# Attention in a two-layer backbone: sink as a PSUM column, two query blocks in one value product

## The chip, the core and the metric

One core of a Trainium2 chip runs the whole program in one launch. The metric is device time in microseconds, the median of several runs. The profile shows one execution.

## The reference, cut to what matters

```python
def _sink_softmax(scores, sink):
    snk = sink[:, :, None]
    m = snk
    for s in scores:
        m = jnp.maximum(m, jnp.max(s, axis=-1))
    ex = [jnp.exp(s - m[..., None]) for s in scores]
    denom = jnp.exp(snk - m)
    for e in ex:
        denom = denom + jnp.sum(e, axis=-1)
    return [e / denom[..., None] for e in ex]

def _window_attn_mixer(h, hc, rope, w_in, w_out, q_norm_w, k_norm_w, sink, need_ctx_out):
    ...
    s_win = jnp.einsum('bnqhgd,bnkhd->bnhgqk', qb, kw).astype(f32) * scale
    s_win = jnp.where(valid[None, :, None, None], s_win, -jnp.inf)
    s_ctx = jnp.einsum('bnqhgd,bkhd->bnhgqk', qb, kc).astype(f32) * scale
    p_win, p_ctx = _sink_softmax([s_win, s_ctx], snk)
    o = (jnp.einsum('bnhgqk,bnkhd->bnqhgd', p_win.astype(v.dtype), vw)
         + jnp.einsum('bnhgqk,bkhd->bnqhgd', p_ctx.astype(vc.dtype), vc))
    y = o.reshape(B, L, D_MODEL) @ w_out
```

512 latent tokens in 4 blocks of 128 attend to the 256 context tokens and, in a window of 128 to either side, to their own and the neighbouring blocks. 16 query heads of 64 share 4 key-value heads. Each head has one sink logit, which enters the softmax's maximum and its denominator and has no value. Everything is float32.

## The kernel before

The program runs layer 0 (retention and mLSTM), its FFN, then layer 1: the attention this text is about, its output projection (`op_out`) and a last FFN. All work is written as generators; `Flow` books each instruction with a price by engine and shape (`Engine`, lines 97 to 133) and lets the generator go on that is due first, and the framework's scheduler sets the final order of each engine's queue when the program is built. So a price in `Engine` moves instructions wherever a shape of that kind occurs: for float32 products other than transposes this is line 115. The products of the adaLN modulation (`ada_round`, tile `ada`, weights of 32 columns, fed by the weight tiles `aw`) are float32 too; those outside the start have 256 columns of data.

The attention runs while the main generator still projects queries (`pt`), norms and rotates them (`norm_rope`, transposes `ntr`, results `qst`); keys are `khh` and `kll` (a high and a low part), values `vt`. The loop `its` has 32 items n: 4 key-value groups g, 2 pairs of heads hp, 4 query blocks j. An item has two heads q.

`attention_p` (lines 1952 to 1983) makes one head's probabilities. A two-bank PSUM tile `sc` (two exist, tag `s2`) takes the scores: columns 256 to 511 the context, from 512 on the two or three key blocks of the window, with two products that add the masks. DVE reduces the negated scores to their minimum with the negated sink, ACT takes the exponential with that as bias and sums it, takes the exponential of the sink logit, DVE adds the two sums and inverts, POOL multiplies the tile `aE` (7 exist) by the inverse.

`attention_o` (lines 1985 to 2033) has the rest. PE transposes the probabilities of both heads, 128 columns at a time, into a bank `atr`; ACT or DVE copies two key blocks of it to a tile `pth`, of which there are 5. An item takes 2 or 3 of them (context blocks, then the window's), so that a pair of query blocks needs all 5. After every second item the value product `ao` runs for the pair (lines 2019 to 2025). Its weights are a key block of `vt`, 64 columns, and its data 256 columns: both heads of one query block. Query block j-1 writes the first 64 partitions of the bank and block j the others, each with as many products as it has key blocks (4 and 5, or 5 and 4):

```python
        for i in range(5):
            for s, prs in enumerate(two):
                if i < len(prs):
                    pe.matmul(po[64 * s:64 * s + 64, 0:256], prs[i][0], prs[i][1], start=(i == 0),
                              stop=(i == len(prs) - 1), tile_position=(0, 64 * s))
```

Four copies of 64x128 on ACT (`oh`, the high part) and four subtractions on DVE (`ol`, the low part) then put it into place for the output projection.

Of the kernel before, what the change touches and what calls it, by code (L numbers as in the profile page):

```python
# [96 lines left out]
class Engine:  # L97
# [5 lines left out]
    def __getattr__(self, op):  # L103
        fn = getattr(self._e, op)

        def call(*a, **k):
            r = fn(*a, **k)  # L107
            n = math.prod(a[0].shape[1:])
            if self._n == "pe":
                if op == "transpose":  # L110
                    cost = 0.11
                else:
                    dt, m = a[1].dtype, math.prod(a[1].shape[1:])
                    if dt == F32:
                        cost = max(0.22, 0.01 + n / 600)
                    elif dt == F32R:
                        cost = max(0.106 if m > 64 else 0.054, n / 2400 + 0.003)
                    else:
                        cost = max(0.04, n / 2400 + 0.003)
            elif self._n == "act":  # L120
                cost = 0.095 + n / 1200
            elif self._n == "dve":
                cost = 0.13 + n / 960
            elif ALU.pow in a:
                cost = 0.3 + n / 6
            else:
                cost = 0.3 + n / 600
            if self._n == "pe" and self._f.cur.name == "main":
                self._f.main = r
            self._f.charge(self._n, cost)  # L130
            return r

        return call
# [10 lines left out]
def kernel(ctx, tc, x, c, cx, c_ctx, ada_w, ada_b, norm_w, ffn_w_in, ffn_w_out, ab_w_in,  # L144
# [48 lines left out]
    def f(ap):  # L193
        return ap.bitcast(F32)
# [1625 lines left out]
    n_aE, n_pt = Count(7), Count(5)  # L1820
# [4 lines left out]
    def start1():  # L1825
# [7 lines left out]
        A["sink8"] = sink8 = mt1("sink8", [P, 16], 1)  # L1833
        nc.scalar.dma_start(sink8, sink[0].partition_broadcast(P))
        A["nsink"] = nsink = mt1("nsink", [P, 16], 1)
        dve.tensor_scalar(nsink, sink8, -1.0, None, ALU.mult)
# [110 lines left out]
    E, halfway = {}, {}  # L1947
# [4 lines left out]
    def attention_p(n, g, hp, j, q):  # L1952
# [9 lines left out]
        ps = psum2("sc")  # L1962
# [8 lines left out]
        st = mt1("ast", [P, 5], 7)  # L1971
        e_ = mt1("aE", [P, 640], 7)
        sc = ps[:, NCX:NCX + nk]

        dve.tensor_scalar(e_[:, 0:nk], sc, -1.0, A["nsink"][:, h:h + 1], ALU.mult, ALU.min, accum_out=st[:, 0:1])
        n_sc[0] += 1
        act.activation(e_[:, 0:nk], sc, AF.Exp, bias=st[:, 0:1], accum_out=st[:, 1:2])
        act.activation(st[:, 2:3], A["sink8"][:, h:h + 1], AF.Exp, bias=st[:, 0:1])
        yield
        dve.tensor_tensor(st[:, 3:4], st[:, 1:2], st[:, 2:3], ALU.add)  # L1980
        dve.reciprocal(st[:, 4:5], st[:, 3:4])
        pool.tensor_tensor(e_[:, 0:nk], e_[:, 0:nk], st[:, 4:5].to_broadcast([P, nk]), ALU.mult)
        E[n, q] = e_

    def attention_o(n, g, hp, j):

        kt = 2 * g + hp
        j0, j1 = window(j)
        nb = 2 + j1 - j0
# [6 lines left out]
        yield spend((n_pt, -(-nb // 2)))  # L1996
        pts = []
        for i0 in range(0, nb, 2):
            m = min(2, nb - i0)
            pst = psum("atr", "pj")  # L2000
            for i in range(m):
                for q in range(2):
                    pe.transpose(pst[:, 256 * i + P * q:256 * i + P * q + P],
                                 E[n, q][:, P * (i0 + i):P * (i0 + i) + P], ident)
            pv = pst[:, 0:256 * m].rearrange("p (i n) -> p i n", i=m)
            th = mt1("pth", [P, 2, 256], 5)
            (act.copy if i0 != 2 else dve.tensor_copy)(th[:, 0:m, :], pv)
            pts += [th[:, i, :] for i in range(m)]
            if i0 + 2 < nb:
                flow.cur.t = 0.0  # L2010
                yield
        n_tr[0] += 1
        n_aE.n += 2
        chs = [0, 1] + [2 + jj for jj in range(j0, j1)]
        halfway[n] = [(A["vt"][:, ch, 64 * g:64 * g + 64], pts[i]) for i, ch in enumerate(chs)]
        if j % 2 == 0:
            return
        yield lambda: n_av[0] == n - 1
        po = psum("ao", "mx")
        two = halfway[n - 1], halfway[n]  # L2020
        for i in range(5):
            for s, prs in enumerate(two):
                if i < len(prs):
                    pe.matmul(po[64 * s:64 * s + 64, 0:256], prs[i][0], prs[i][1], start=(i == 0),
                              stop=(i == len(prs) - 1), tile_position=(0, 64 * s))
        n_pt.n += sum(-(-len(prs) // 2) for prs in two)
        n_av[0] += 2
        quads = [(slice(64 * q, 64 * q + 64), slice(P * (j - 1 + s), P * (j + s)),
                  po[64 * s:64 * s + 64, P * q:P * q + P]) for s in range(2) for q in range(2)]
        for r, od, p_ in quads:  # L2030
            act.copy(oh_[kt // 3][r, kt % 3, od], p_)
        for r, od, p_ in quads:
            dve.tensor_tensor(ol_[kt // 3][r, kt % 3, od], p_, f(oh_[kt // 3][r, kt % 3, od]), ALU.subtract)

    def start_attention():
        for n, it in enumerate(its):
            for q in range(2):
                flow.add(attention_p(n, *it, q), 10, f"attention p {n} {q}")
            flow.add(attention_o(n, *it), 10, f"attention o {n}")
# [364 lines left out]
```

## Time and profile before

| | us |
|---|---|
| median of 3 runs (1773.08 to 1778.31) | 1775.1 |
| the profiled execution | 1772.4 |
| its span | 1770.6 |
| PE busy | 1704.5 |
| DVE busy | 1248.5 |
| ACT busy | 774.0 |
| POOL busy | 302.7 |

The span runs from the first to the last instruction of the profiled execution. PE is the engine of the matrix products and transposes; a float32 product shows as two rows there. A busy share is a mean over stages with different limits, so the share of one stage is taken from its own stretch. Starts of neighbouring rows say more of PE than the length of one row, as products are pipelined. In the groups, "idle before" is the time for which the engine stood still ahead of such an instruction, with what ended most of it.

### The profile page before, as it was taken

To read this page: it belongs to the slowest core of one execution; us is meant where nothing else is said; L and a number is where in the kernel's file an instruction comes from. 1 tells how busy PE (TensorE), PEld (TensorE's weight loads), DVE (VectorE), ACT (ScalarE), POOL (GpSimd) and SP (SyncE) were. 2 spreads that over 40 slices of the span, in tenths; PEclk is the share of its full clock that TensorE was granted. 3 is DMA by queue.
4 is the path that set the end of the run, shared out by engine and by line. 5 is a ranking of instruction groups with operands and counts; after the bars stand their busy time and mean duration, and the time that the engine had idled before them with its cause. 6 is when DMAs were issued, how large, how long until landed. Compare 5 with 4: busy or idle time off the path is not lost.

```text
span 1770.6 us, 31626 instructions
## 1 busy us (share of the span) xinstructions
PE 1704.5 (96%) x12738; PEld 1553.7 (88%) x12738; DVE 1248.5 (71%) x2224; ACT 774.0 (44%) x1502; POOL 302.7 (17%) x307
## 2 busy tenths in 40 slices
PE   7899999999998999999999999998999999999998
PEld 5799899999878998989999997897667999999998
DVE  5845365756598886867567566878886687778775
ACT  4532344433324533433334334545675553434343
POOL 4212120201123001010000103435553300000000
PEclk8999999999999999999999999999999999999999
DMA  9511111011476248484656755221002523323335
GB/s 345 197 52 48 37 37 48 25 39 52 161 237 204 83 144 177 126 187 141 166 134 175 167 176 151 84 73 49 1 1 80 171 72 97 119 83 108 108 89 150
DMA packets 230326, 203.36 MB, mean 115 GB/s; under 512 B 8172, under 2 KB 207268, under 8 KB 230180
## 3 DMA queue, kind: packets, MB, share of 16 engines
q1 hardware_dynamic: 222468, 178.20, 33.0%
q0 software_dynamic: 5760, 18.88, 5.5%
q10 hardware_dynamic: 1952, 4.27, 0.7%
q8 instruction: 100, 1.64, 0.4%
q14 instruction: 46, 0.38, 0.1%
HBM read 178.25 MB, written 23.07 MB: 114 GB/s over the span
## 4 chain that ended last, share of the span: by engine, by line
PE 64%; issue 13%; DVE 11%; DMA 6%; ACT 3%; POOL 1%; SPq 0%; POOLq 0%; ACTq 0%; DVEq 0%
PE pf L107 21%; PE pu L107 11%; PE pt L107 10%; PE pg L107 4%; DMA wr<-in_ffn_w_in_dram 3%; PE sc L107 3%; PE pc L107 3%; PE ao L107 2%; DVE wl L107 2%; PE mo L107 2%; PE atr L107 2%; DMA xs<-stage 1%; DVE acc L107 1%; PE ro L107 1%; DMA aw<-in_ada_w_dram 1%
## 5 line engine op out<-in xcount | busy, mean ns | idle before, releaser
L107 PE MATMUL pf<-fu,wh 128*128 128x512 f32 (+1 forms) x1152 | 290.6, 343 | 8.3 <-DVE xt L107 3.8
L107 PEld LDWEIGHTS pf<-fu,wh 128*128 128x128 f32 x1152 | 196.6, 188 | 37.8 <-issue 4.4
L107 ACT CAST wh<-wr 128x1024 fp32r<-128x1024 f32 (+1 forms) x144 | 143.6, 1001 | 179.4 <-PE pf L107 77.7
L107 DVE TENSOR_TENSOR wl<-wr,wh 128x1024 fp32r<-128x1024 f32 (+1 forms) x144 | 174.3, 1212 | 64.6 <-ACT wh L107 62.9
L107 PE MATMUL pf<-fu,wl 128*128 128x512 f32 (+1 forms) x576 | 195.3, 341 | 0.4 <-DVE wl L107 0.4
L107 DVE TENSOR_TENSOR wl<-ws,wh 128x1024 fp32r<-128x1024 f32 x80 | 97.4, 1221 | 57.4 <-ACT wh L107 49.6
L107 PE MATMUL pu<-g,wh 128*128 128x256 f32 x704 | 130.4, 283 | 0.0
L107 ACT CAST xh<-wr 128x1024 fp32r<-128x1024 f32 x84 | 78.4, 946 | 114.3 <-DMA wr<-in_ffn_w_in_dram 61.3
L107 PE MATMUL pc<-g,xh 128*128 128x256 f32 x672 | 122.4, 282 | 1.2 <-ACT stage L107 0.8
L107 ACT CAST wh<-ws 128x1024 fp32r<-128x1024 f32 x80 | 83.3, 1049 | 88.2 <-PE pu L107 45.9
L107 PEld LDWEIGHTS pf<-fu,wl 128*128 128x128 f32 x576 | 108.2, 188 | 14.1 <-DVE wl L107 0.6
L107 DVE SCALAR_TENSOR_TENSOR acc<-aw,cmod,acc 128x1024 f32<-128x1024 f32 x90 | 118.0, 1336 | 0.3
L107 PE MATMUL pu<-hT,wh 128*128 128x256 f32 x640 | 115.4, 281 | 0.0
L107 PEld LDWEIGHTS pu<-g,wh 128*128 128x128 f32 x704 | 108.9, 190 | 1.2 <-issue 1.2
L107 PEld LDWEIGHTS pc<-g,xh 128*128 128x128 f32 x672 | 103.4, 189 | 2.1 <-ACT stage L107 1.2
L107 DVE TENSOR_TENSOR xl<-wr,xh 128x1024 fp32r<-128x1024 f32 x84 | 91.6, 1095 | 18.8 <-ACT xh L107 18.8
L107 PE MATMUL pu<-g,wl 128*128 128x256 f32 x352 | 99.4, 284 | 0.8 <-DVE wl L107 0.8
L107 PEld LDWEIGHTS pu<-hT,wh 128*128 128x128 f32 x640 | 97.6, 188 | 0.6 <-ACT hT L107 0.2
L1774 POOL DMA_DIRECT2D xs<-stage x32 | 27.9, 871 | 393.9 <-ACT stage L107 375.1
L107 PE MATMUL pc<-g,xl 128*128 128x256 f32 x336 | 94.3, 281 | 0.0
L107 PE MATMUL pu<-hT,wl 128*128 128x256 f32 x320 | 88.0, 281 | 0.9 <-DVE wl L107 0.9
L107 PE MATMUL pt<-wh,hh 128*128 128x256 f32 x288 | 83.5, 291 | 3.6 <-ACT hh L107 2.2
(383 smaller groups left out, 4914.7 us busy)
## 6 DMA issues: line engine op xcount, KB each, us to landing
wr<-in_ffn_w_in_dram SPq DMA_DIRECT2D x88, 512.0 KB, 3.9
aw<-in_ada_w_dram SPq DMA_DIRECT2D x84, 512.0 KB, 5.0
wr<-in_ab_w_in_dram SPq DMA_DIRECT2D x32, 512.0 KB, 4.0
wr<-in_ffn_w_out_dram SPq DMA_DIRECT2D x32, 512.0 KB, 4.3
xs<-stage POOLq DMA_DIRECT2D x32, 384.0 KB, 6.2
wr<-in_ffn_w_out_dram SPq DMA_DIRECT2D x32, 384.0 KB, 4.1
wr<-in_ab_w_out_dram SPq DMA_DIRECT2D x16, 512.0 KB, 4.7
wr<-in_attn_w_out_dram SPq DMA_DIRECT2D x16, 512.0 KB, 4.1
```

Source lines behind the costliest of these rows:

```text
L107: r = fn(*a, **k)
L1774: nc.gpsimd.dma_start(xs2[k // 2, :, NT * (k % 2):NT * (k % 2) + NT], stage[0][:, k % 2], accum_op=ALU.add)
```

## The change

**The sink.** Two `sc` tiles are taken once and stand through the whole attention, one for each head q of an item. At j = 0, when a head begins, ACT copies the sink logits of this and the next head into columns 255 and 256; the first score product then overwrites column 256. The exponential reads one column more, from 255 on, so that its sum holds the sink's share. The exponential of the sink by itself and DVE's add are gone. In `aE` the probabilities begin at column 8, the sink's share lies in column 7.

**The value product.** The transposed probabilities of two query blocks go into common tiles: `ptc` the two context blocks, `ptm` the two middle key blocks, which both query blocks see, `pte` the outer key block that one of them sees. The evictions write them with a stride, so that for one head the two query blocks lie side by side. A product now has 256 columns of one head, both query blocks, and head q writes row half q; the outer block has 128 columns. There are two of each tile, counted by `n_pt`. One copy of 128x256 and one subtraction of that shape move the result.

**The price.** A float32 product with weights of at most 64 columns and 256 or more of data is booked at 0.21 us.

```diff
--- before.py
+++ after.py
@@ -112,7 +112,7 @@
                 else:
                     dt, m = a[1].dtype, math.prod(a[1].shape[1:])
                     if dt == F32:
-                        cost = max(0.22, 0.01 + n / 600)
+                        cost = max(0.22, 0.01 + n / 600) if m > 64 or n < 256 else 0.21
                     elif dt == F32R:
                         cost = max(0.106 if m > 64 else 0.054, n / 2400 + 0.003)
                     else:
@@ -1817,7 +1817,7 @@
     A = {}
     kdone, vdone, qdone = set(), set(), set()
     khh, kll, qst, oh_, ol_ = [], [], [], [None] * 3, [None] * 3
-    n_aE, n_pt = Count(7), Count(5)
+    n_aE, n_pt = Count(7), Count(2)
 
     def mt1(name, shape, bufs, dt=F32):
         return A["pool"].tile(shape, dt, tag=name, name=nm(name), bufs=bufs)
@@ -1830,10 +1830,11 @@
         A["nwb"] = nwb = mt1("nwb", [P, 2, 64], 1)
         nc.scalar.dma_start(nwb[:, 0, :], q_norm_w[0].partition_broadcast(P))
         nc.scalar.dma_start(nwb[:, 1, :], k_norm_w[0].partition_broadcast(P))
-        A["sink8"] = sink8 = mt1("sink8", [P, 16], 1)
-        nc.scalar.dma_start(sink8, sink[0].partition_broadcast(P))
+        A["sink8"] = sink8 = mt1("sink8", [P, 18], 1)
+        pool.memset(sink8[:, 16:18], 0.0)
+        nc.scalar.dma_start(sink8[:, 0:16], sink[0].partition_broadcast(P))
         A["nsink"] = nsink = mt1("nsink", [P, 16], 1)
-        dve.tensor_scalar(nsink, sink8, -1.0, None, ALU.mult)
+        dve.tensor_scalar(nsink, sink8[:, 0:16], -1.0, None, ALU.mult)
         dve.tensor_scalar(nwb[:, 0, :], nwb[:, 0, :], 0.125, None, ALU.mult)
         A["rtab"] = rtab = mt1("rtab", [P, 2, 2, 4, 64], 1)
         for i in range(2):
@@ -1944,7 +1945,7 @@
 
     its = [(g, hp, j) for g in range(4) for hp in range(2) for j in range(4)]
     n_sc, n_tr, n_av = [0], [0], [0]
-    E, halfway = {}, {}
+    E, pair = {}, [None]
 
     def window(j):
         return max(0, j - 1), min(4, j + 2)
@@ -1959,7 +1960,10 @@
         yield lambda: {0, 1, 2} <= kdone and (g, j // 2) in qdone and n_sc[0] == 2 * n + q
         yield spend((n_aE, 1))
         qt = qst[h // 3][:, h % 3, P * j:P * j + P]
-        ps = psum2("sc")
+        ps = A["sc"][q]
+        if j == 0:
+
+            act.copy(ps[:, NCX - 1:NCX + 1], A["sink8"][:, h:h + 2])
         pw = ps[:, 512:512 + nw]
         group(ps[:, NCX:512], [(qt, kh_[:, 0:NCX]), (qt, kl_[:, 0:NCX])])
         pe.matmul(pw, qt, kh_[:, a:a + nw], start=True, stop=False)
@@ -1968,71 +1972,79 @@
             pe.matmul(pw[:, 0:P], identb, mgt, start=False, stop=(j == 3))
         if j < 3:
             pe.matmul(pw[:, nw - P:nw], identb, mlt, start=False, stop=True)
-        st = mt1("ast", [P, 5], 7)
-        e_ = mt1("aE", [P, 640], 7)
-        sc = ps[:, NCX:NCX + nk]
-
-        dve.tensor_scalar(e_[:, 0:nk], sc, -1.0, A["nsink"][:, h:h + 1], ALU.mult, ALU.min, accum_out=st[:, 0:1])
+        st = mt1("ast", [P, 3], 7)
+        e_ = mt1("aE", [P, 648], 7)
+
+        dve.tensor_scalar(e_[:, 8:8 + nk], ps[:, NCX:NCX + nk], -1.0, A["nsink"][:, h:h + 1], ALU.mult, ALU.min,
+                          accum_out=st[:, 0:1])
         n_sc[0] += 1
-        act.activation(e_[:, 0:nk], sc, AF.Exp, bias=st[:, 0:1], accum_out=st[:, 1:2])
-        act.activation(st[:, 2:3], A["sink8"][:, h:h + 1], AF.Exp, bias=st[:, 0:1])
+        act.activation(e_[:, 7:8 + nk], ps[:, NCX - 1:NCX + nk], AF.Exp, bias=st[:, 0:1], accum_out=st[:, 1:2])
         yield
-        dve.tensor_tensor(st[:, 3:4], st[:, 1:2], st[:, 2:3], ALU.add)
-        dve.reciprocal(st[:, 4:5], st[:, 3:4])
-        pool.tensor_tensor(e_[:, 0:nk], e_[:, 0:nk], st[:, 4:5].to_broadcast([P, nk]), ALU.mult)
+        dve.reciprocal(st[:, 2:3], st[:, 1:2])
+        pool.tensor_tensor(e_[:, 8:8 + nk], e_[:, 8:8 + nk], st[:, 2:3].to_broadcast([P, nk]), ALU.mult)
         E[n, q] = e_
 
     def attention_o(n, g, hp, j):
+
 
         kt = 2 * g + hp
         j0, j1 = window(j)
-        nb = 2 + j1 - j0
+        s = j % 2
         yield lambda: (n, 0) in E and (n, 1) in E and n_tr[0] == n and len(vdone) == 3
         if j == 0 and kt % 3 == 0:
             yield spend((slots, 2))
             slots.n += 2
             oh_[kt // 3] = big([P, 3, NL], F32R, "oh")
             ol_[kt // 3] = big([P, 3, NL], F32R, "ol")
-        yield spend((n_pt, -(-nb // 2)))
-        pts = []
-        for i0 in range(0, nb, 2):
-            m = min(2, nb - i0)
+        if s == 0:
+            yield spend((n_pt, 1))
+            pair[0] = (mt1("ptc", [P, 2, 2, 2, P], 2), mt1("ptm", [P, 2, 2, 2, P], 2), mt1("pte", [P, 2, P], 2))
+        tc_, tm, te = pair[0]
+        edge = 2 if j < 2 else 1
+        mid = 2 * (j // 2)
+        parts = [(tc_, [0, 1]), (tm, [2 + mid, 3 + mid])]
+        if j in (1, 2):
+            parts.append((te, [2 + edge]))
+        for t, chs in parts:
+            m = len(chs)
             pst = psum("atr", "pj")
-            for i in range(m):
+            for i, ch in enumerate(chs):
+                col = 8 + P * (ch if ch < 2 else ch - j0)
                 for q in range(2):
-                    pe.transpose(pst[:, 256 * i + P * q:256 * i + P * q + P],
-                                 E[n, q][:, P * (i0 + i):P * (i0 + i) + P], ident)
-            pv = pst[:, 0:256 * m].rearrange("p (i n) -> p i n", i=m)
-            th = mt1("pth", [P, 2, 256], 5)
-            (act.copy if i0 != 2 else dve.tensor_copy)(th[:, 0:m, :], pv)
-            pts += [th[:, i, :] for i in range(m)]
-            if i0 + 2 < nb:
+                    pe.transpose(pst[:, 256 * i + P * q:256 * i + P * q + P], E[n, q][:, col:col + P], ident)
+            if m == 1:
+                act.copy(te, pst[:, 0:256].rearrange("p (q n) -> p q n", q=2))
+                break
+            pv = pst.rearrange("p (i q n) -> p i q n", i=2, q=2)
+            (act.copy if t is tc_ else dve.tensor_copy)(t[:, :, :, s, :], pv)
+            if t is tc_ or len(parts) == 3:
                 flow.cur.t = 0.0
                 yield
         n_tr[0] += 1
         n_aE.n += 2
-        chs = [0, 1] + [2 + jj for jj in range(j0, j1)]
-        halfway[n] = [(A["vt"][:, ch, 64 * g:64 * g + 64], pts[i]) for i, ch in enumerate(chs)]
-        if j % 2 == 0:
+        if s == 0:
             return
         yield lambda: n_av[0] == n - 1
         po = psum("ao", "mx")
-        two = halfway[n - 1], halfway[n]
+        v_ = lambda ch: A["vt"][:, ch, 64 * g:64 * g + 64]
+        se = 1 if j == 1 else 0
         for i in range(5):
-            for s, prs in enumerate(two):
-                if i < len(prs):
-                    pe.matmul(po[64 * s:64 * s + 64, 0:256], prs[i][0], prs[i][1], start=(i == 0),
-                              stop=(i == len(prs) - 1), tile_position=(0, 64 * s))
-        n_pt.n += sum(-(-len(prs) // 2) for prs in two)
+            for q in range(2):
+                o = po[64 * q:64 * q + 64, 0:256]
+                at = dict(start=(i == 0), stop=(i == 4), tile_position=(0, 64 * q))
+                if i < 4:
+                    t, ch = (tc_, i) if i < 2 else (tm, mid + i)
+                    pe.matmul(o, v_(ch), t[:, i % 2, q].rearrange("p s n -> p (s n)"), **at)
+                else:
+                    pe.matmul(o[:, P * se:P * se + P], v_(2 + edge), te[:, q, :], **at)
+        n_pt.n += 1
         n_av[0] += 2
-        quads = [(slice(64 * q, 64 * q + 64), slice(P * (j - 1 + s), P * (j + s)),
-                  po[64 * s:64 * s + 64, P * q:P * q + P]) for s in range(2) for q in range(2)]
-        for r, od, p_ in quads:
-            act.copy(oh_[kt // 3][r, kt % 3, od], p_)
-        for r, od, p_ in quads:
-            dve.tensor_tensor(ol_[kt // 3][r, kt % 3, od], p_, f(oh_[kt // 3][r, kt % 3, od]), ALU.subtract)
+        od = slice(P * (j - 1), P * (j + 1))
+        act.copy(oh_[kt // 3][:, kt % 3, od], po[:, 0:256])
+        dve.tensor_tensor(ol_[kt // 3][:, kt % 3, od], po[:, 0:256], f(oh_[kt // 3][:, kt % 3, od]), ALU.subtract)
 
     def start_attention():
+        A["sc"] = [psum2("sc") for _ in range(2)]
         for n, it in enumerate(its):
             for q in range(2):
                 flow.add(attention_p(n, *it, q), 10, f"attention p {n} {q}")
```

How instructions move. First PE's queue before, inside the attention, where the first value product of a pair (`ao`) stands; `sc` are scores, `atr` transposes:

```order
L107 MATMUL sc_13939<-mlt,identb 128x128
L107 MATMUL atr_13917<-cst,aE_13869 128x128
L107 MATMUL ao_13951<-pth_13878,vt_11808 64x256
L107 MATMUL atr_13917<-cst,aE_13898 128x128
L107 MATMUL atr_13917<-cst,aE_13869 128x128
L107 MATMUL atr_13917<-cst,aE_13898 128x128
```

The product that needs only the first query block's transposes stands by itself between transposes. Further on in the same pair, still before:

```order
L107 MATMUL ao_13951<-pth_13922,vt_11808 64x256
L107 MATMUL ao_13951<-pth_13878,vt_11808 64x256
L107 MATMUL ao_13951<-pth_13922,vt_11808 64x256
L107 MATMUL ao_13951<-pth_13885,vt_11808 64x256
L107 MATMUL sc_13986<-khh_11805,qst_12262 128x256
L107 MATMUL sc_13986<-kll_11807,qst_12262 128x256
L107 MATMUL sc_13986<-khh_11805,qst_12262 128x256
L107 MATMUL sc_13986<-kll_11807,qst_12262 128x256
L107 LDWEIGHTS identb
L107 MATMUL sc_13986<-mgt,identb 128x128
L107 MATMUL ao_13951<-pth_13929,vt_11808 64x256
L107 MATMUL ao_13951<-pth_13885,vt_11808 64x256
```

The other products of the pair follow in two stretches, parted by a head's scores. PE's queue in the changed kernel, at a pair of the same kind:

```order
L107 MATMUL atr_13777<-cst,aE_13723 128x128
L107 MATMUL atr_13777<-cst,aE_13750 128x128
L107 MATMUL ao_13793<-ptc_13726,vt_11809 64x256 x4
L107 MATMUL sc_12261<-khh_11806,qst_12265 128x256
L107 MATMUL sc_12261<-kll_11808,qst_12265 128x256
L107 MATMUL sc_12261<-khh_11806,qst_12265 128x256
L107 MATMUL sc_12261<-kll_11808,qst_12265 128x256
L107 LDWEIGHTS identb
L107 MATMUL sc_12261<-mgt,identb 128x128
L107 MATMUL ao_13793<-ptm_13727,vt_11809 64x256 x4
L107 MATMUL ao_13793<-pte_13728,vt_11809 64x128 x2
L107 MATMUL atr_13831<-cst,aE_13762 128x128
```

All ten products of a pair stand in two stretches, four products and then four and two, parted by a head's scores. The third place is SP's queue in the output projection of layer 0, where `aw` are weights of the modulation and `wr` weights of the projection. Before:

```order
L768 DMA aw_5300<-in_ada_w_dram 128x1024
L506 DMA wr_5296<-in_ab_w_out_dram 128x8x128
L768 DMA aw_5326<-in_ada_w_dram 128x1024
L768 DMA aw_5343<-in_ada_w_dram 128x1024
L506 DMA wr_5322<-in_ab_w_out_dram 128x8x128
```

In the changed kernel:

```order
L506 DMA wr_5296<-in_ab_w_out_dram 128x8x128
L768 DMA aw_5316<-in_ada_w_dram 128x1024
L768 DMA aw_5339<-in_ada_w_dram 128x1024
L506 DMA wr_5335<-in_ab_w_out_dram 128x8x128
L768 DMA aw_5343<-in_ada_w_dram 128x1024
```

The `wr` load has moved ahead of an `aw` load; further such exchanges follow up to the start of that layer's FFN, and none of the loads is added or dropped.

## Rows read from the trace of the kernel before

**Rows 1.** The page, parts 1 and 4: busy us by engine; chain by engine.
```profile
PE 1704.5 (96%) x12738; PEld 1553.7 (88%) x12738; DVE 1248.5 (71%) x2224; ACT 774.0 (44%) x1502; POOL 302.7 (17%) x307
...
PE 64%; issue 13%; DVE 11%; DMA 6%; ACT 3%; POOL 1%; SPq 0%; POOLq 0%; ACTq 0%; DVEq 0%
```

**Rows 2.** Two stretches: length, busy us of PE, PEld, DVE, ACT, POOL; clock; DMA.
```profile
1181.00:1231.00 50.00, 44.20 (x343) 41.50 (x342) 47.21 (x101) 28.64 (x67) 28.66 (x21) 0.93 0.22 64
...
1275.00:1309.05 34.05, 32.57 (x234) 22.30 (x234) 28.73 (x90) 25.86 (x80) 18.38 (x17) 1.00 0.01 2
```

**Rows 3.** The chain that ended last, attention stage: start us, us, what.
```profile
1194.03 1.17 DVE ast L107
...
1274.99 1.32 PE sc L107 x11
...
1309.04 1.30 PE sc L107 x11
```

**Rows 4.** PE in order of time: start us, us, operation, tiles, shapes, count.
```profile
1231.18 2.38 PE L107 MATMUL ao<-pth,vt 128*64 128x256 f32 x18
1233.49 0.39 PE L107 MATMUL sc<-khh,qst 128*128 128x256 f32 x1
...
1286.33 0.94 PE L107 MATMUL atr<-cst,aE 128*128 128x128 f32 x7
1287.02 0.36 PE L107 MATMUL sc<-khh,qst 128*128 128x256 f32 x1
...
1287.90 1.08 PE L107 MATMUL ao<-pth,vt 128*64 128x256 f32 x8
1288.92 0.33 PE L107 MATMUL atr<-cst,aE 128*128 128x128 f32 x1
1289.17 1.08 PE L107 MATMUL ao<-pth,vt 128*64 128x256 f32 x8
...
1296.87 1.51 PE L107 MATMUL ao<-pth,vt 128*64 128x256 f32 x8
1298.31 0.39 PE L107 MATMUL sc<-khh,qst 128*128 128x256 f32 x1
```

**Rows 5.** Groups, 1275 to 1309.05 us: count, busy us, mean ns, idle before.
```profile
L107 PE MATMUL atr<-cst,aE 128*128 128x128 f32 x72 | 11.6, 282 | 0.5 <-DVE pth L107 0.2 <-ACT pth L107 0.2
L107 PE MATMUL sc<-khh,qst 128*128 128x256 f32 (+1 forms) x33 | 10.6, 341 | 1.0 <-ACT aE L107 1.0
...
L107 DVE TENSOR_TENSOR ast<-ast 128x1 f32<-128x1 f32 x17 | 6.0, 355 | 1.8 <-ACT ast L107 1.7
...
L107 ACT CAST oh<-ao 64x128 fp32r<-64x128 f32 x19 | 4.9, 260 | 1.7 <-PE ao L107 1.6
L107 ACT ACTIVATE ast<-sink,ast 128x1 f32<-128x1 f32 x16 | 4.6, 288 | 0.0
L107 DVE TENSOR_TENSOR ol<-ao,oh 64x128 fp32r<-64x128 f32 x16 | 4.6, 287 | 0.2
```

**Rows 6.** Groups: `ast` on DVE, 1181 to 1231 us; three shapes, whole span.
```profile
L107 DVE TENSOR_TENSOR ast<-ast 128x1 f32<-128x1 f32 x10 | 3.3, 335 | 0.0
L107 DVE RECIPROCAL ast<-ast 128x1 f32<-128x1 f32 x10 | 1.4, 152 | 0.1
...
L107 ACT COPY pth<-atr 128x256 f32<-128x256 f32 x16 | 5.9, 367 | 0.7 <-PE atr L107 0.5
L107 ACT ACTIVATE dn<-mo 128x4 f32<-128x4 f32 x24 | 4.2, 177 | 20.1 <-PE mo L107 14.8 <-DVE hd L107 5.4
...
L107 DVE TENSOR_TENSOR hfull<-pt,cst 128x256 f32<-128x256 f32 x32 | 11.6, 417 | 4.1 <-PE pt L107 4.0
```

**Rows 7.** In order of time: one add on DVE, POOL's multiply beside it.
```profile
1290.44 0.94 DVE L107 TENSOR_TENSOR ast<-ast 128x1 f32<-128x1 f32 x1 [0.50 <-ACT ast L107]
...
1290.11 1.25 POOL L107 TENSOR_TENSOR aE<-aE,ast 128x640 f32<-128x640 f32 x1 [0.38 <-DVE ast L107]
```

**Rows 8.** The chain in the output projection of layer 0.
```profile
511.12 6.72 DMA aw<-in_ada_w_dram
```

## Prediction

> **What bounds the kernel now.** First the page [rows 1]: PE counts as busy 96% of the span, and the chain that ended last runs over PE for 64% of it. So a microsecond off another engine is worth something only where PE waits for it. The change lies in one stage, so next the table of stretches [rows 2]. While the queries are still being projected (1181 to 1231 us) DVE is busy 47.2 of 50 us; in a stretch of pure attention (1275 to 1309) PE has 32.6 of 34 us at a granted clock of 1.00, DVE 28.7, ACT 25.9, POOL 18.4. The chain [rows 3] says the same: before 1231 it runs over DVE, one piece of it the one-element add on `ast`; from 1231 nearly all its pieces are PE's. It also gives the period: the eleven score rows that open a key-value group start at 1274.99 and again at 1309.04, so 16 heads (four pairs of query blocks) take 34.05 us. In that stretch PE's own idle time is small and shared out: 1.0 us before a score, 0.5 before transposes [rows 5]. The attention stage is thus bound first by PE, which the value product loads, and by DVE only while the queries run.
>
> **The value products.** What one costs is read from stretches of `ao` rows, start to the start of the next row [rows 4]. 18 in a row: 1231.18 to 1233.49, 2.31 us. Eight: 1287.90 to 1288.92, 1.02. The last eight of a pair with a longer second block: 1296.87 to 1298.31, 1.44. A product has two rows, and products for different row halves of the output run beside each other, so a stretch lasts as many steps as its busier half has rows: 10, 4 and 6. The differences give 0.215 us a step and 0.15 us beside them for each stretch. Entering costs the same again: the first `ao` row after a lone transpose starts 0.25 us after it, where transposes follow each other every 0.10. So about 0.30 us a stretch.
>
> Before, the halves are the two query blocks of a pair, which have four and five key blocks, and the first product needs the first block's transposes alone, so the scheduler sets it by itself. A pair is cut 2, 8, 8 or 2, 8, 6, 2 rows: 10 steps for two pairs of a group and 12 for the other two, 44 in all, in 13 stretches. That is 44 x 0.215 + 13 x 0.30 = 13.4 us a group. After, the halves are the two heads. Each half has four products of 256 columns (8 steps) and one of 128 (two short steps; between half a step and a whole one each, I take half: 0.215 for both), always even, and the order now cuts a pair into two stretches. That is 4 x (8 x 0.215 + 0.215 + 2 x 0.30) = 10.1 us. So 3.2 us a group. PE is the bound here, so it counts in full; the first pair already stood in one stretch of 18 rows. 15 pairs of 4 to a group: 15 / 4 x 3.22, **-12.1 us**.
>
> **The sink.** 64 one-column exponentials leave ACT (288 ns each), 64 one-element adds leave DVE (mean 355 ns), and POOL's normalising waits for that add no more [rows 5]. One more column in each exponential is 1 in 513 to 641 and costs nothing that can be seen. In the pure stretch all of this lies beside PE. In the query stretch DVE is the chain, and there ten adds take 3.3 us [rows 6]. How much of that comes back? One add of one element took 0.94 us and ended at 1291.38; POOL's multiply of a whole `aE` tile ran from 1290.11 to 1291.36 [rows 7]. So a long add is a wait for POOL's instruction, and it goes with the add: **-3.3 us**. The Trainium skill (SBUF — State Buffer, "Who interferes with whom") says that a DVE instruction with two SBUF inputs contends with a GpSimd instruction that reads SBUF, while one with at most one such input does not; the trace agrees, for the reciprocal, with one input, takes 152 ns a time in the same stretch [rows 6]. By that rule the whole 3.3 us goes; by the add's own work, taken as the reciprocal's 152 ns, 1.5 would.
>
> Sixteen copies of two columns into the score tiles are new on ACT. The nearest rows are 177 ns (four columns out of PSUM) and 288 ns (one column) [rows 5, 6]: 2.8 to 4.6 us of ACT in all, beside 64 x 0.288 = 18.4 taken away. A copy stands behind the exponential that last read its tile, and the next score of that tile waits for it. PE has transposes and value products in between, so I count nothing; without that cover it is a rival below.
>
> **Evictions and buffers.** Per pair, four 64x128 copies on ACT (260 ns) and four subtractions on DVE (287) [rows 5] become one each of 128x256, for which rows of that shape say 367 and 417 ns [rows 6]: 16 x 0.67 = 11 us of ACT and 16 x 0.73 = 12 of DVE go. In a group DVE falls from 28.7 to some 20 us and ACT from 25.9 to 19, against PE's 30 or so, hence no gain by itself. What it buys, with two pairs of transposes in flight where five `pth` tiles held one, is shorter waits. In a group PE waits 1.0 + 0.5 us for ACT, DVE and the like; 52 of 64 heads come after 1231, which is 3.25 groups, 4.9 us. I take half, **-2.4**, since the value products also reach their operands sooner; the ends are none and all of it.
>
> **The planner's price.** A float32 product with at most 64 columns of weights and 256 or more of data is now booked at 0.21 us, where 0.437 stood. That holds for the `ada` rounds of 256 columns too, so the output projection of layer 0 and the first units of its FFN are written in another order: SP issues an `aw` load behind a `wr` load that it preceded. There the chain already shows a 6.7 us wait for `aw` [rows 8]. One such wait more, or one less, bounds the effect from both sides, and PE covers most of it; I take 0. In the last FFN some products change places and none is added or dropped: 0.
>
> **Sum:** -12.1 - 3.3 - 2.4 = -17.8. The profiled execution took 1772.4 us (span 1770.6), so 1754.6; it lies 2.7 us below the median of the runs (1775.1), which puts the time at **1757 us**.
>
> **Rivals.**
> 1. *The waits go altogether.* For it: DVE and ACT keep 10 us of slack a group, and POOL, the slowest to answer after that, waits for the add no more. Then all 4.9 us of waiting go, and the query stretch gains as much again as I counted, since PE waits for DVE through it, and 4 us come from the new order in layer 0: 12.1 + 4.9 + 6.6 + 4 = 27.6, hence 1747.5. Chance 0.2.
> 2. *PE waits for what it got ahead of.* Two score tiles serve all heads, and each is free only after DVE's reduction and ACT's exponential, both of which stand behind copies in their queues. If PE reaches the scores sooner than these, half of the 12.1 us is handed back as waiting and nothing else comes: -6, 1769. Against it: the trace shows a single wait of 1.0 us for `aE` in 34 us [rows 5]. Chance 0.15.
> 3. *Slower: the sink copy gates the scores.* At the start of each head pair ACT must write a column into a tile before PE may. If a copy stands behind the eviction of a value product, PE waits for the eviction (0.37), the copy (up to 0.29) and their hand-overs, about 1.2 us, 16 times: +19 against the -15 that remain without the halved waits, so about 1779. It decides if ACT reaches the copy later than PE the score. In the new order one of the two copies per pair of heads does stand behind an eviction, but six transposes and a score follow the product on PE. The Trainium skill (PSUM — Partial Sum Buffer, "PSUM bank collisions raise a hardware error") wants accesses kept apart by bank, not by address; by that rule PE would wait for the copy even if the columns were apart. Chance 0.05.
> 4. *The heads do not run beside each other.* Then a pair takes 16 steps and four short ones, 3.9 us where it took 2.4: +24 over 16 pairs, less 6 for the fewer stretches and 5.7 for the rest of the sum: about 1787. Against it: with the same halves, blocks do it now [rows 4]. Chance 0.02.
> The other 0.03 is layer 0 losing more than I bound it by.
>
> **How the numbers follow.** The forecast has 0.55: 1750 to 1764. The range takes in rival 1 and most of rival 2, down to 1745 and up to 1771; outside lie rivals 3 and 4, part of rival 2 and a gain beyond rival 1. About 0.3%, 5.3 us, is what can be told from no change here. Faster than 1769.8: the forecast, rival 1 and two thirds of rival 2, 0.85. Within 5.3 us: the rest of rival 2 and small losses, 0.09. Slower: 0.06.
>
> **What would show it.** Right: the group's period falls from 34.05 to about 30 us; `ao` stands in stretches with even halves, two to a pair, and a stretch of eight still takes 1.02 us; DVE and ACT are busy about 20 and 19 us a group; DVE's `ast` rows are reciprocals alone, 0.16 us each; the chain between 1190 and 1230 us has no `ast` row of more than 0.2 us. The forecast is wrong if the period stays above 33 us, if a score often waits for ACT's copy of the sink, or if the stages ahead of 1110 us differ by more than 4 us.

## The result, and the profile after

The changed kernel takes 1762.0 us (median of 4 runs) where the kernel before took 1774.9 beside it: a ratio of 0.9924, 95% interval 0.9908 to 0.9941. That is faster by 0.76%, 13.5 us (10 to 16 by the interval). The forecast was 1757, 18 us faster, and its range held the result. The profiled execution took 1761.6 us, its span 1759.8; before 1772.4 and 1770.6.

The page after, parts 1 and 4; these lines answer to [rows 1]:

```profile
PE 1688.9 (96%) x12770; PEld 1551.6 (88%) x12770; DVE 1213.0 (69%) x2112; ACT 754.0 (43%) x1406; POOL 305.7 (17%) x308
...
PE 63%; issue 14%; DVE 10%; DMA 6%; ACT 4%; POOL 2%; SPq 0%; POOLq 0%; ACTq 0%; DVEq 0%
```

Of this almost nothing can be learned: the shares hardly moved. The stage itself has to be read. The query stretch and one key-value group after, as a table of stretches with the columns of [rows 2]:

```profile
1193.30:1240.00 46.70, 44.13 (x359) 41.81 (x358) 45.54 (x94) 28.38 (x60) 30.41 (x21) 0.96 0.23 68
1284.78:1314.85 30.07, 29.34 (x243) 21.87 (x242) 20.89 (x60) 20.09 (x52) 18.18 (x16) 1.00 0.01 1
```

The group's length comes from the chain after, in the same stage; start us, us, what:

```profile
1284.78 0.72 PE sc L107 x6
1285.50 0.44 PE atr L107 x4
1285.94 1.01 PE ao L107 x8
1286.96 0.26 PE atr L107
1287.22 0.71 PE sc L107 x6
1287.93 1.23 PE ao L107 x12
...
1290.26 0.90 DVE aE L107 x2
...
1291.19 0.89 ACT aE L107 x2
...
1292.12 0.81 PE sc L107 x5
...
1314.85 0.72 PE sc L107 x6
```

The same six score rows stand at 1284.78 and, two half groups later, at 1314.85: 30.07 us a group, where [rows 3] gave 34.05. DVE fell from 28.7 to 20.9 us a group, ACT from 25.9 to 20.1. The value product of a pair stands in two stretches, eight rows in 1.01 us and, four of them short, twelve in 1.23. New on this group's chain are pieces of DVE and ACT between two scores: the reduction, the exponential, then the next score of that tile. In the group of [rows 3] only one exponential stood there and no reduction, though elsewhere in the attention the chain before has such pieces too. The line before:

```profile
1299.52 0.54 ACT aE L107
```

The groups of that stretch, to be held against [rows 5]; count, busy us, mean ns, idle before:

```profile
L107 PE MATMUL atr<-cst,aE 128*128 128x128 f32 x73 | 12.0, 281 | 0.5 <-DVE ptm L107 0.5
L107 PE MATMUL sc<-khh,qst 128*128 128x256 f32 x25 | 8.2, 341 | 0.3
L107 DVE RECIPROCAL ast<-ast 128x1 f32<-128x1 f32 x16 | 2.6, 160 | 4.7 <-ACT aE L107 4.7
L107 DVE TENSOR_TENSOR ol<-ao,oh 128x256 fp32r<-128x256 f32 x4 | 1.7, 423 | 0.2
L107 ACT CAST oh<-ao 128x256 fp32r<-128x256 f32 x4 | 1.4, 362 | 0.0
L107 ACT COPY sc<-sink 128x2 f32<-128x2 f32 x4 | 0.7, 170 | 0.1
```

PE's waits ahead of scores and transposes are 0.3 + 0.5 us a group, where they were 1.0 + 0.5. The sink's copy takes 170 ns.

The other half of the story lies 600 us earlier, in layer 0. Three stretches of 10 us at the start of its FFN, the changed kernel:

```profile
550.00:560.00 10.00, 3.64 (x27) 3.26 (x27) 5.54 (x9) 10.00 (x17) 4.08 (x5) 0.96 0.80 270
560.00:570.00 10.00, 10.00 (x62) 10.00 (x63) 10.00 (x17) 3.23 (x7) 2.49 (x2) 0.70 0.41 122
570.00:580.00 10.00, 8.75 (x74) 8.54 (x74) 6.97 (x14) 5.09 (x8) 3.65 (x1) 1.00 0.00 0
```

PE issues 163 rows there. With layer 0 in the order of before (the first experiment) the same 30 us are:

```profile
550.00:560.00 10.00, 6.61 (x39) 6.24 (x40) 6.34 (x11) 10.00 (x19) 3.07 (x5) 0.84 0.94 301
560.00:570.00 10.00, 10.00 (x85) 10.00 (x85) 10.00 (x14) 1.92 (x5) 2.55 (x2) 0.98 0.39 114
570.00:580.00 10.00, 10.00 (x87) 10.00 (x86) 6.91 (x15) 5.15 (x8) 1.70 (x1) 1.00 0.01 2
```

That is 211 rows, 48 more. At 0.117 us a row (85 rows in 10 us) the change is 5.6 us behind by 580. What PE waited for stands in its groups from 536 to 592 us, the changed kernel:

```profile
L107 PE MATMUL pu<-g,xh 128*128 128x256 f32 x64 | 14.1, 312 | 5.3 <-ACT g L107 4.0 <-DVE g L107 1.4
L107 PE MATMUL nbc<-cst,rs 128*128 128x128 f32 x12 | 1.9, 292 | 1.3 <-POOL rs L107 1.3
```

With layer 0 in the old order PE does not wait ahead of `nbc`, and ahead of `pu` it waits half as long:

```profile
L107 PE MATMUL pu<-g,xh 128*128 128x256 f32 x64 | 13.1, 300 | 2.8 <-ACT g L107 1.8 <-DVE g L107 1.0
```

So PE stands 2.5 us longer before the first products of the FFN (`pu`), whose operand `g` comes from ACT and DVE: ACT's rows `bb`, which `g` is made from, begin 3 us later. It stands 1.3 us longer before the broadcast (`nbc`) of the second half of the norm. And the granted clock takes about 1.6 us more: by the stretches above (1 - 0.96 + 1 - 0.70) x 10 = 3.4 us, against 1.8 with the old order. Together that is about 5.4 of the 5.6 us. Pieces of the chain there, the changed kernel:

```profile
551.67 1.28 ACT bb L107 x3
...
561.62 6.69 issue
568.34 5.32 POOL rs L107
573.71 0.71 PE nbc L107 x4
```

In the old order PE is at work up to `nbc`:

```profile
548.69 0.75 ACT bb L107 x2
...
566.32 8.01 PE pu L107 x67
574.33 0.44 PE nbc L107 x4
```

There POOL's `rs` took 1.70 us and ended at 572.2; in the change it began 2.1 us sooner, took 5.3 and ended at 573.7, with no product left for PE to put beside it. Why it took so much longer, and which of the exchanged loads holds ACT back, no run shows.

### The profile page after: what moved, and what is told of

Its sections match the earlier page's. It is cut to its first block, busy times and chain, and to the rows that moved or that the text cites. A ratio compares the mean times of both kernels' runs of the same rounds, so it can differ in the third digit from the quotient of the medians.

```text
span 1759.8 us, 31421 instructions
## 1 busy us (share of the span) xinstructions
PE 1688.9 (96%) x12770; PEld 1551.6 (88%) x12770; DVE 1213.0 (69%) x2112; ACT 754.0 (43%) x1406; POOL 305.7 (17%) x308
## 4 chain that ended last, share of the span: by engine, by line
PE 63%; issue 14%; DVE 10%; DMA 6%; ACT 4%; POOL 2%; SPq 0%; POOLq 0%; ACTq 0%; DVEq 0%
PE pf L107 20%; PE pu L107 12%; PE pt L107 10%; PE pg L107 4%; PE pc L107 4%; DMA wr<-in_ffn_w_in_dram 3%; PE sc L107 3%; DVE acc L107 2%; PE mo L107 2%; PE ao L107 2%; DVE wl L107 2%; DMA xs<-stage 1%; PE atr L107 1%; PE ro L107 1%; PE kv L107 1%
## 5 line engine op out<-in xcount | busy, mean ns | idle before, releaser
L107 ACT CAST wh<-ws 128x1024 fp32r<-128x1024 f32 x80 | 83.5, 1050 | 94.8 <-PE pu L107 47.8
L107 PEld LDWEIGHTS pf<-fu,wl 128*128 128x128 f32 x576 | 109.0, 189 | 13.5
L107 DVE SCALAR_TENSOR_TENSOR acc<-aw,cmod,acc 128x1024 f32<-128x1024 f32 x90 | 117.9, 1335 | 0.1
L107 DVE TENSOR_TENSOR xl<-wr,xh 128x1024 fp32r<-128x1024 f32 x84 | 91.7, 1096 | 21.5 <-ACT xh L107 21.3
```

## The experiments

All times are set against the kernel before run beside them; "us" is (ratio - 1) x 1773. An interval is about 2.4 us to either side, so two runs can be told apart from some 3.5 us on. The last four columns are read from each run's own trace: the start of the first score `sc`; from there to the last query transpose `ntr` (the query stretch); on to the last score (the pure stretch); on to the first product of the output projection.

| run | ratio | us | first sc | query | pure | rest |
|---|---|---|---|---|---|---|
| before | 1 | 0 | 1181.4 | 48.8 | 117.9 | 9.5 |
| the change | 0.9924 | -13.5 | 1193.3 | 46.4 | 100.5 | 5.7 |
| price for 64 columns | 0.9881 | -21.1 | 1184.5 | 45.3 | 102.4 | 5.7 |
| old price | 0.9879 | -21.5 | 1182.7 | 45.3 | 102.4 | 5.7 |
| one pair in flight | 0.9882 | -20.9 | 1183.8 | 45.3 | 102.4 | 5.7 |
| new price alone | 1.0042 | +7.4 | 1196.1 | 49.5 | 116.7 | 7.9 |
| `ada` at 0.37 | 0.9881 | -21.1 | 1184.4 | 44.6 | 102.7 | 5.7 |
| `ada` at 0.30 | 0.9929 | -12.6 | 1190.9 | 46.4 | 100.9 | 5.7 |
| value part alone | 0.9929 | -12.6 | 1183.5 | 49.1 | 104.9 | 7.8 |
| sink part alone | 0.9965 | -6.2 | 1183.4 | 45.3 | 116.2 | 7.7 |
| add, two operands | 0.9946 | -9.6 | 1184.5 | 50.8 | 104.3 | 7.1 |
| add, one operand | 0.9930 | -12.4 | 1184.8 | 50.1 | 104.2 | 7.1 |
| add, read by nobody | 0.9887 | -20.0 | 1187.6 | 45.4 | 102.3 | 5.7 |
| ACT's exponential again | 0.9922 | -13.8 | 1185.8 | 47.8 | 105.5 | 7.1 |

### Where did the 12 us ahead of the attention come from?

The price, limited to the shape that the change needs:

```diff
-                        cost = max(0.22, 0.01 + n / 600) if m > 64 or n < 256 else 0.21
+                        cost = max(0.22, 0.01 + n / 600) if m != 64 or n < 256 else 0.21
```

> The changed kernel, with the new price for weights of exactly 64 columns alone, so that the modulation products (32 columns) are booked at 0.437 us as before. Theory A (the price moved layer 0 and cost about 12 us there, the attention gained about 23): the first score starts at 1181 to 1182 us as before, the attention keeps its 152.6 us from the first score to the projection, total about 1751 us, 11 below the change. Rival B (the attention ran faster only because it began 12 us later with more of its loads and projections done): the first score moves back to 1181, but the attention takes some 164 us again and the total stays near 1762. Rival C (the loss ahead of the attention has another source, for instance the places of the tiles in memory): first score still at 1193, total 1762.

1752.9 us (ratio interval 0.9868 to 0.9895): theory A. The first score moves back by 9 us of the 12 and the attention keeps its speed, 153.4 us from the first score to the projection against 152.7 in the change. Rivals B and C fall. This version is faster than both kernels, than the change by 0.9881/0.9924, some 7.6 us.

The old price line as a whole:

> The changed kernel with the old price line everywhere. Theory A: layer 0 as before, first score at 1181 to 1182 us. The value products are booked at 0.437 us instead of 0.21, so the order inside the attention may differ; if the price has no worth there, 1751 us like the run with 64 columns alone, and if the order it gives is worth something, up to 4 us more (1755). Rival B: 1762. Rival C: first score at 1193, total 1762.

1752.0 us. The order of every engine is row for row that of the run before, so the price of the value products had no worth of its own: the planner chose the same attention at 0.437 and at 0.21 us. The two runs are one program, and show how well a time repeats.

The kernel before with the new price line and nothing else:

> The kernel before with the new price line and nothing else. Theory A: the loss of layer 0 comes with the price alone, first score at about 1193 us and total 1775 + 12 = 1787, a few us less if the attention's order gains from the truer price. Rivals B and C: under B the attention makes the late start good, 1775 to 1779; under C nothing happens ahead of the attention, 1775.

1780.7 against 1773.2 (1.0029 to 1.0055): slower by the price alone, 7.4 us where 12 were expected. The trace of before begins its attention earlier than all others with that order (1181.4; the others lie from 1182.7 to 1187.6), so the 11.9 us between the two first traces were some 3 too many; and the trace of the new price alone is of its slowest execution (1783.9). It holds 156 PE rows from 550 to 580 us, about as few as the change.

Which of the reordered places costs? The price of an `ada` product was moved in steps:

```diff
-  ... if m != 64 or n < 256 else 0.21
+  ... if m > 64 or n < 256 else 0.21 if m == 64 else 0.37      (second run: 0.30)
```

> On the version with the price for 64 columns alone (1752.9 us): the modulation products booked at 0.37 us. At this price SP's loads stand in the old order and PE's rows differ from that version only in the first input projections, in the attention and in the last FFN (there as in the change). Theory A (the exchanges of the modulation's and projection's loads in layer 0 cost the time): first score at 1181 to 1185 us as before, total 1751 to 1755. Rival D (the rows that changed places early, in the input projection of layer 0, already cost it): first score near 1193, total about 1762.

> The same with 0.30 us. Now the output projection of layer 0 and the first units of its FFN stand as in the change, with the wr and aw loads exchanged, while the second exchange, late in that FFN, is not made yet. Theory A: the first exchange brings the step that the trace of the change shows at 540 to 590 us, +5.7 to 7, and the second the step at 1000 to 1020 us, about +3.7; so this run ends at 1758 to 1760, between the version with 64 columns alone (1752.9) and the change (1762). Rival E (the second exchange costs it all): 1752 to 1754. Rival F (the first costs it all): 1761 to 1763.

At 0.37 us the time stays, 1752.3; rival D falls, the early rows are harmless. At 0.30 it is 1761.1: rival F by the medians, the first exchange (in the output projection and the first FFN units) brings all of it that can be told from noise. The trace of that run:

```profile
550.00:560.00 10.00, 4.73 (x34) 4.05 (x32) 5.44 (x8) 9.24 (x16) 3.90 (x5) 0.88 0.84 276
560.00:570.00 10.00, 9.22 (x64) 9.22 (x65) 10.00 (x16) 4.05 (x9) 1.85 (x3) 0.78 0.47 144
570.00:580.00 10.00, 7.69 (x52) 7.49 (x52) 7.49 (x14) 2.74 (x5) 4.49 (x1) 0.83 0.00 0
```

150 rows instead of 211. Ahead of the attention the change differs from that run in the order of its rows from 738 to 788 us alone, the second exchange. Its trace is 0.8 us ahead of that run's at 1000 us and 3 behind from 1020 on; but at that same place runs with one and the same order step against one another by up to 4 us. So what the second exchange costs, if anything, stays open.

What an `ada` round really takes stands in the chain after, four products in eight rows:

```profile
1027.22 0.57 PE ada L107 x8
```

So 0.14 us each, and the new 0.21 is nearer to it than the old 0.437. The planner does not lose by a wrong price here: it lost when the price came nearer to what the trace shows.

### Which part of the attention gains, and how?

Each part alone, on the kernel before, with the old price:

> The kernel before with the new value products, their tiles and evictions, without the sink's part and with the old price. By the prediction's terms: -12.1 for the products and -2.4 for the waits, 1760.5. If the value part brings all that the attention gained, 1752. If the score tiles and DVE's adds hold PE back once its products are shorter (the sink's part is then needed to reap them), 1765 or more.

> The kernel before (1773.2 us in the last session) with the sink's part alone: standing score tiles, the column, no add, the old value products, the old price. By the prediction's term 3.3 us off, 1770, in the query stretch (48.8 us before, 45.5 then). If the sink's part is worth beside the old products what the stages of the other runs leave for it (about 8 us, of which 4 in the query stretch), 1765. If it pays in the pure stretch only where PE is short, 1769 with the stretch after the last query transpose at 117 to 118 us as before.

The value part brings 12.6 us (0.9915 to 0.9943), 13.0 of them in the pure stretch by the trace and nothing in the query stretch: products and waits together, as booked. The sink part brings 6.2 alone (0.9953 to 0.9978), and on top of the value part 21.1 - 12.6 = 8.5, where 3.3 were booked. In the query stretch it is 3.5 us as forecast; the rest lies in the pure stretch (1.7 beside the old products, 2.5 beside the new) and at its end.

One pair of transposes in flight instead of two:

```diff
-    n_aE, n_pt = Count(7), Count(2)
+    n_aE, n_pt = Count(7), Count(1)
```

> On the version with the price for 64 columns alone (1752.9 us): one pair of transposes in flight instead of two (the counter only; the tiles stay). By my term of halved waits 2.4 us go, 1755. If the second pair covers the turn from a pair's value product to the next pair's transposes (15 times some 0.5 to 1 us), 1760 to 1768. If it is worth nothing, 1753.

1752.4 us, and again the same program row for row: the planner had never started a second pair. Whether one set of tiles would do as well was not tried.

Then the two instructions that the sink's column replaced were put back, one by one, on the version with the price for 64 columns (`ast` gets a fourth column for it):

```diff
-        dve.reciprocal(st[:, 2:3], st[:, 1:2])
+        dve.tensor_tensor(st[:, 3:4], st[:, 1:2], A["sink8"][:, 16:17], ALU.add)
+        dve.reciprocal(st[:, 2:3], st[:, 3:4])
```

> On the version with the price for 64 columns alone (1752.9 us): DVE's one-element add of two SBUF operands is back between the exponential's sum and the reciprocal, adding a zero; the sink stays a column of the scores. Theory A (the gain of the sink's part is the add, which waits for POOL's multiply): the query stretch (first score to last query transpose, 45.3 us now) goes back to about 49, the pure stretch gains some 2 us, total 1757 to 1761. Rival (the gain is ACT's one-column exponential): all but 1 to 2 us stay, 1754. The add takes a mean of 0.3 us or more under A.

With one operand the new line is `dve.tensor_scalar(st[:, 3:4], st[:, 1:2], 0.0, None, ALU.add)`:

> The same, but the add has one SBUF operand (an immediate zero is added), so the instruction, its place and the hop stay and the second operand goes. If the add costs by waiting for POOL over its second operand, it takes about 0.15 us like the reciprocal and the total stays within 1 to 2 us of 1752.9, the query stretch at 45 to 46.5 us. If an instruction more in DVE's queue is what costs, it is as slow as the add with two operands, 1757 to 1761.

And that same line behind the reciprocal, which reads `st[:, 1:2]` again:

> On the version with the price for 64 columns alone (1752.9 us): the one-operand add is there again, but behind the reciprocal and read by nobody; the other instructions stand almost in the same order. If DVE's busy time is what the add costs (64 x 0.15 us, ten or so of them in the query stretch), 1.5 us come back in the query stretch and up to 9 in all: 1754 to 1761. If it costs by its place in the chain from the exponential to the normalised probabilities (the reciprocal then falls behind the next reduction), nothing comes back here: 1752 to 1754, query stretch 45 to 46 us.

The groups of `ast` on DVE; count, then min/median/max ns and first and last start. With two operands:

```profile
L107 DVE TENSOR_TENSOR ast<-ast,sink x64: 134/158/1256, 1192.5 to 1342.2; 128x1 f32<-128x1 f32 x64
```

With one:

```profile
L107 DVE TENSOR_SCALAR ast<-ast x64: 134/151/156, 1192.8 to 1341.1; 128x1 f32<-128x1 f32 x64
```

So with the second operand the add at times takes up to 1.26 us, and with one never more than 0.16; PE's order is the same in both runs. The Trainium skill (SBUF — State Buffer, "Who interferes with whom") says that a DVE instruction with two SBUF inputs contends with a GpSimd instruction that reads SBUF, and one with at most one such input, outside its two-port modes, does not. This pair of runs agrees. But the add with one operand costs almost as much time: 8.7 us against 11.5, which cannot be told apart, query stretch 50.1 and 50.8. Read by nobody it costs 1.1, within the interval. So most of the price is not the wait for POOL, nor DVE's 64 x 0.15 us; it is the place in the chain of a head. DVE in order of time, the version without the add:

```profile
1192.36 0.16 DVE L107 TENSOR_SCALAR qss<-qss 128x8 f32<-128x8 f32 x1
1192.43 0.21 DVE L107 RECIPROCAL ast<-ast 128x1 f32<-128x1 f32 x2
1192.56 0.86 DVE L107 TENSOR_SCALAR_CACHE_REDUCE aE<-sc,nsink 128x640 f32<-128x640 f32 x1
```

With the add of one operand:

```profile
1192.74 0.16 DVE L107 TENSOR_SCALAR qss<-qss 128x8 f32<-128x8 f32 x1
1192.82 0.20 DVE L107 TENSOR_SCALAR ast<-ast 128x1 f32<-128x1 f32 x2
1192.94 0.87 DVE L107 TENSOR_SCALAR_CACHE_REDUCE aE<-sc,nsink 128x640 f32<-128x640 f32 x1
...
1193.74 0.21 DVE L107 RECIPROCAL ast<-ast 128x1 f32<-128x1 f32 x2
```

Between the adds and the reciprocals the scheduler set a reduction of 0.87 us. From the end of the exponential's sum to the end of the reciprocal a head's mean over all 64 is 0.65 us without the add, 0.66 with the idle one, 1.16 and 1.36 with the add in the chain; for the first 12 heads, nearly all in the query stretch, 1.46, 1.51, 2.74 and 2.91. What the added instruction does is thus mostly to send the next one to the back of a short queue. PE's order changes with it (hardly with the idle one), so how much of the loss is the later arrival and how much the order that the scheduler made of it is not separated.

Last, ACT's one-column exponential, read by nobody:

```diff
+        act.activation(st[:, 3:4], A["sink8"][:, h:h + 1], AF.Exp, bias=st[:, 0:1])
```

> On the version with the price for 64 columns alone (1752.9 us): ACT takes the one-column exponential of the sink again behind each large one, and nobody reads it. If ACT's 64 x 0.29 us are covered, as I counted, 1752 to 1754. If ACT stands in the loop of scores, reduction and exponential now that PE is shorter, part of 18 us shows: 1757 to 1765, in the stretch after the last query transpose (102.4 us now).

1759.0 us: 7.3 come back, and the counted cover is not there. PE's groups from 1232 to 1337 us, first without it, then with it:

```profile
L107 PE MATMUL sc<-khh,qst 128*128 128x256 f32 x102 | 32.5, 340 | 1.5 <-ACT aE L107 0.9
```

```profile
L107 PE MATMUL sc<-khh,qst 128*128 128x256 f32 x100 | 32.2, 344 | 5.1 <-ACT aE L107 4.9
```

PE waits 4.9 us for ACT's large exponential where it waited 0.9. Here too the order of PE's rows moved, and the query stretch lost 2.5 us. This cost and the add's do not add up: either alone gives back about what both together do in the run of the value part alone, which also has no standing score tiles. What those tiles are worth by themselves was not tried.

## Why the prediction was right, and where it was not

The sum was -17.8 us; by the ratios it is -12.6 (value part) - 8.5 (sink on top of it) + 7.6 (price) = -13.5. Faster was right. That 1762 lies so near to 1757 is luck: the sink gave 5.2 us more than booked, and the price took 7.6 that were not booked.

- **The value products, -12.1, and the waits, -2.4.** The value part alone measured -12.6 against -14.5, equal within its interval. A pair's two stretches take 2.24 us and a turn before and behind them as booked, and the two short steps of each half together 0.22 (0.215 was the choice between the bounds). PE's waits fell from 1.5 to 0.8 us a group, half as booked; but not by "two pairs of transposes in flight where five `pth` tiles held one": a second pair is never in flight. What shortened them was not tested further than that ACT's exponential, put back, lengthens them.
- **The sink, -3.3: the step that was mis-sized.** The query stretch gave 3.5 us, so the number held, and its reason fell for the most part: "a long add is a wait for POOL's instruction, and it goes with the add". A short add costs almost as much. The step "in the pure stretch all of this lies beside PE" failed outright: on top of the value part 2.5 us came in the pure stretch and 2 at its end, and beside the old products it was already 1.7 and 1.8. This suggests that the loop of score, reduction, exponential and next score lay on PE's path in part before the products got shorter. That 288 ns of ACT per head stand in it is shown: with the exponential back PE waits 4.9 us for ACT where it waited 0.9. This is the mechanism of rival 2, which showed as a limit of the gain only when the sink's work was put back.
- **The planner's price, 0: the step that failed.** "One such wait more, or one less, bounds the effect from both sides, and PE covers most of it; I take 0." It cost 7.6 us (7.4 on the kernel before), no less than the bound of 6.7, and PE covered none of it. Nor was it a wait for `aw` in the output projection, as the bound assumed (the chain of the change waits 5.5 us there, against 6.7): most of it lies at the start of the FFN, where PE stood still for the operand `g` and for the norm, and then ran part of its products at the lower clock. The prediction had named this as what would show it wrong (stages ahead of 1110 us off by more than 4 us), and by that sign it was wrong there: the first score came 11.9 us later in the traces. It had left it the last 0.03 of the chances, but no term in the forecast.
- **Sink copies, 0.** Right: 164 ns in the median, and in the whole trace after one engine once waited 0.2 us for such a copy. Rival 3 falls with it, rival 4 with the 30.07 us, and rival 1 with the 0.8 us of waiting a group that are left.
- **What would show it.** The period of 30 us, DVE and ACT near 20, the stretches of `ao`, reciprocals of 0.16 us and a query stretch whose chain has no `ast` piece above 0.15 us all came as written.

## What to carry to other kernels

A price in a planner is an input to an order, not a cost: a line meant for one shape also reprices every other shape that matches it, and the order far from the change must be timed, not argued. When an instruction is taken out of a chain from one engine to another and back, count the queue that its successor falls behind, not its own 0.15 us. When the bound engine gets shorter, work of a neighbour that counted as covered has to be costed anew against the new period.

## What the runs showed of the hardware that was not expected

After PE's near idle stretch at 550 to 560 us (3.6 of 10 busy) the granted clock of the next 10 us was 0.70 in the change, 62 rows against 85 at 0.98: between the two levels, so part of it at 1.2 GHz and part at 2.4. With the old order the clock fell too, less long and mostly before 560 us (0.84, 6.6 of 10 busy). Over both stretches the change lost 1.6 us more to the clock, of the 5.6 lost by 580 us, beside 3.8 us more of standing still: here a stall of PE cost more than its own length.
